# A third buffer for the modulation columns, and the gate weights of the linear attention in their stage's pool

## The chip, the core and the metric

The kernel runs on one core of a Trainium2 chip. The metric is device time in microseconds; of the kernel before there are three runs: 2583.49, 2584.60 and 2589.62, median 2584.60. One further execution was taken by the hardware profiler: 2585.34 us, of which 2583.5 us lie between its first and its last instruction (the span).

## The reference

A decoder trunk of two layers, float32, 256 tokens of width 2048. Cut to what matters here:

```python
c_act = silu(c)
for l in range(2):
    mod = c_act @ w_mod[l] + b_mod[l]                    # 2048 x 12288, one row
    shift1, scale1, gate1, shift2, scale2, gate2 = split(mod, 6)
    h = rms_norm(x, norm1_gain[l]) * (1 + scale1) + shift1
    x = x + gate1 * token_mixer(h, w_in[l], gla_w_gk[l], ..., w_out[l])
    h = rms_norm(x, norm2_gain[l]) * (1 + scale2) + shift2
    x = x + gate2 * (silu(h @ w_gate[l]) * (h @ w_up[l])) @ w_down[l]
return rms_norm(x, final_norm_gain)
```

The token mixer projects h with w_in and runs three mixers on the columns: a gated linear attention (whose gates are `lr @ gla_w_gk + gla_b_gk`, with lr of 16 columns), a sliding-window attention and a gated delta rule. Their outputs together go through w_out.

## The kernel before

Tokens stand in two blocks of 128 partitions (`blk`). Every large product is a `stream` (L293) of jobs. A job is one block of 128 rows of a weight matrix with up to 1024 of its columns (512 KB): `load` (L313) brings it into a `raw` tile (three buffers, L109), ACT rounds it to `wh` (L330), DVE forms the remainder `wl` (L331), and `products` (L342) multiplies it with both blocks of tokens, three matmuls of 512 columns for each block and half: twelve, all at L358. In some stages the weights are used whole, without rounding, and then land in the tiles raw, wh and wl in turn.

Beside this runs the modulation, which is a single row and so no matrix product: `mod_segment` (L201) cuts each of the six parts into segments of 1024 columns. A step (L208) loads 128 rows of such a segment, 512 KB, into an `mraw` tile of the pool `modp` (two buffers, L110; the load is L220), and one DVE instruction (L223) adds it, times c_act, into an accumulator `acc` (two buffers). A segment has 16 steps, which add one after another; 320 steps use mraw. The first two parts of layer 0 go through smaller tiles of other pools instead (`early`). `finish` (L228) sums each segment over the partitions with TensorE: for shift and scale by transposes (L248) and a DVE reduction (L250); for the gates it first takes two more `mraw` tiles, one for each half of 512 columns:

```python
t = tl(modp, [P, 2, 512], "mraw", F32R)
A.activation(t[:, 0], src, AF.Copy)
V.tensor_tensor(t[:, 1], src, t[:, 0].bitcast(F32), ALU.subtract)
ps = tl(psf, [P, 512], "fin")
for i in range(2):
    TE.matmul(ps, ones_r, t[:, i], start=i == 0, stop=i == 1)
```

These tiles come free when their products (L238) are through.

The text of the kernel says when a step is due: after each job, `tick` (L273) takes steps from a queue at a rate of the stage (L50 to L57: 2.0 a job beside w_out in layer 0, 0.4 and 0.25 beside the feed-forward products). The order in which each engine runs its instructions is set at build time by a scheduler: it walks the program with its own estimates of durations, lets an instruction go ahead of the text when its data and its buffer are there, and writes one fixed order for each engine. Every load is issued by SP, in one such order; a load that waits for its buffer holds back those behind it. DVE, ACT and TensorE too run in order.

The layer's shape: projection with w_in, with the delta rule and the window attention woven in; then the linear attention `gla` (L739), w_out (with `add_gated`, L928), the second norm (`norm`, L427, transposes at L444, scale and shift at L447), and the feed-forward part: products for chunks 0 to 5 in pairs of gate and up (32 jobs a pair), two halves of 24 jobs with w_down, chunks 6 to 10, and two halves of 20 jobs. A gate product's eviction is L1134, that of an up product L1138, that of w_down L929.

Before, the gate weights (`wgk`, 16 x 256) are loaded by `load_small` (L464) at a layer's start into the pool `kp`, which lives through the whole kernel. A tile `ones` of float32 ones (L163) serves a sum in the delta rule (L594) and is rounded by ACT into `ones_r` (L166) for the products L238.

Of the kernel before, what the change touches and what calls it, by code (L numbers as in the profile page):

```python
# [10 lines left out]
F32 = mybir.dt.float32  # L11
# [4 lines left out]
AF = mybir.ActivationFunctionType  # L16
# [3 lines left out]
P = 128  # L20
D = 2048
T = 256
# [81 lines left out]
def trunk(ctx: ExitStack, tc, x, cT, pos, small, consts, b_mod, w_mod, w_in, w_gk, w_out,  # L104
# [2 lines left out]

    kp = ctx.enter_context(tc.tile_pool(name="kp", bufs=1))
    rawp = ctx.enter_context(tc.tile_pool(name="rawp", bufs=3))  # L109
    modp = ctx.enter_context(tc.tile_pool(name="modp", bufs=2))  # L110
    wsp = ctx.enter_context(tc.tile_pool(name="wsp", bufs=3))
    accp = ctx.enter_context(tc.tile_pool(name="accp", bufs=2))
    gatep = ctx.enter_context(tc.tile_pool(name="gatep", bufs=2))
# [9 lines left out]
    def nm(s):  # L123
        uid[0] += 1
        return f"{s}_{uid[0]}"

    def tl(pool, shape, tag, dt=F32, bufs=None):
        return pool.tile(shape, dt, tag=tag, name=nm(tag), bufs=bufs)
# [5 lines left out]
    def bank(tag="mm"):  # L134
        if tag == "any":
            which[0] += 1
            tag = "ga" if which[0] % 3 == 0 else "mm"
        return tl(psm, [P, 512], tag, bufs=1 if tag == "ga" else 2)

    V, A, G, TE, SY = nc.vector, nc.scalar, nc.gpsimd, nc.tensor, nc.sync  # L140
# [17 lines left out]
    def cst(name):  # L158
        o, w = CONST_AT[name]
        return ct[:, o:o + w] if o < N_FULL else masks[:, o - N_FULL:o - N_FULL + w]  # L160

    ident = cst("ident")
    ones = tl(kp, [P, P], "ones")  # L163
    G.memset(ones, 1.0)
    ones_r = tl(kp, [P, P], "ones_r", F32R)
    A.activation(ones_r, ones, AF.Copy)  # L166
    eps_t = tl(kp, [P, 1], "eps")
    G.memset(eps_t, EPS)
    half = tl(kp, [P, 16], "half")
# [287 lines left out]

    scr = [None, None]

    small_t, wgk_t = {}, {}  # L460
    gains = tl(kp, [P, DEPTH, 2 * KD], "gains")
    SY.dma_start(gains, small[:, :, :2 * KD].rearrange("l p n -> p l n"))

    def load_small(l):  # L464
        small_t[l] = tl(kp, [P, SMALL_W], "small")
        SY.dma_start(small_t[l], small[l][:, 2 * KD:])
        wgk_t[l] = tl(kp, [16, 256], "wgk")
        SY.dma_start(wgk_t[l], w_gk[l])

    def sm(l, name):  # L470
        o, w = SMALL[name]
# [57 lines left out]
    def gdn(l, pool, pc, zg, cbca):  # L529
# [3 lines left out]
        for gi, name in enumerate("qkv"):  # L533
            for c2 in range(2):
                ps = bank()
# [49 lines left out]
        ps = bank()  # L585
        for ni, name in enumerate("qk"):
            for c2 in range(2):
                sq = tl(pool, [P, 2, T], "g")
                A.activation(sq, hat[name, c2], AF.Square)
                for c in range(2):  # L590
                    for blk in range(NB):
                        n = ni * 8 + blk * 4 + c2 * 2 + c
                        TE.matmul(ps[:, n:n + 1], sq[:, c, blk * P:(blk + 1) * P],
                                  ones[:, 0:1], start=True, stop=True)  # L594
        ss = tl(smp, [P, 16], "qkss")
        V.tensor_scalar(ss, ps[:, :16], EPS, None, ALU.add)
        norms = tl(smp, [P, 8], "knorm")
# [12 lines left out]
        for blk in range(NB):  # L610
            ps = bank()
# [12 lines left out]
        for blk in range(NB):  # L624
# [4 lines left out]
            ps = bank()  # L629
# [7 lines left out]
            if blk == 0:  # L637
                ps = bank()
# [6 lines left out]
            else:  # L645
                ps = bank()
# [5 lines left out]
            ps = bank()  # L652
            for h in range(4):
                TE.matmul(ps[:, h * P:(h + 1) * P], ch("k", h, blk), ch("k", h, blk),
                          start=True, stop=True)
# [3 lines left out]
            ps = bank()  # L659
            for h in range(4):  # L660
                TE.matmul(ps[:, h * P:(h + 1) * P], ch("k", h, blk), ch("q", h, blk),
                          start=True, stop=True)
# [10 lines left out]
        for m in LEVELS[1:]:  # L673
            for blk in range(NB):
                ps = bank()
# [5 lines left out]
                ps = bank()  # L681
# [13 lines left out]
        for blk in range(NB):  # L695
            rhs = v_tok[blk]
            if blk == 1:
                ps = bank()
# [7 lines left out]
            ps = bank()  # L706
# [5 lines left out]
            if blk == 0:  # L712
                ps = bank()
# [5 lines left out]
                ps = bank()  # L719
# [4 lines left out]
            else:  # L724
                ps = bank()
# [5 lines left out]
                ps = bank()  # L731
# [6 lines left out]

    def gla(l, pool, qk_tok, v_tok, zg, lr):  # L739

        chan = []
        for i in range(2):
            ps = bank("ga")
# [10 lines left out]
        ps = bank("ga")  # L754
        for blk in range(NB):
            TE.transpose(ps[:16, blk * P:(blk + 1) * P], lr[blk], ident)
        lrT = tl(pool, [16, T], "lrT", bufs=1)
        A.activation(lrT, ps[:16, :T], AF.Copy)
        ps = bank("ga")
        for blk in range(NB):  # L760
            TE.matmul(ps[:, blk * T:(blk + 1) * T], lrT[:, blk * P:(blk + 1) * P], wgk_t[l],
                      start=True, stop=True)
        z = tl(pool, [P, NB, T], "a")
        V.tensor_tensor(z, ps.rearrange("p (b c) -> p b c", b=NB), bc(sm(l, "b_gk"), NB, 1),
# [7 lines left out]
        ps = bank("ga")  # L772
# [62 lines left out]
        for blk in range(NB):  # L835
            ps = bank("ga")
            for h in range(4):
                o = ps[:, h * P:(h + 1) * P]
                if blk == 1:
                    TE.matmul(o, cross[:, h % 2, h // 2], v_tok[0][:, h * P:(h + 1) * P],  # L840
                              start=True, stop=False)
                TE.matmul(o, Am[h % 2][:, h // 2, blk], v_tok[blk][:, h * P:(h + 1) * P],
                          start=blk == 0, stop=True)
# [105 lines left out]
    def layer(l):  # L949
        wi, wo = w_in[l], w_out[l]  # L950
        load_small(l)
        blocks, at = [], 0
        for n in (K_BLOCKS if l == 0 else (KD,)):
# [90 lines left out]
        for bi, ks in enumerate(blocks):  # L1044
            first, last = bi == 0, bi == len(blocks) - 1
            rate[1] = RATE_LAST if last and l == 0 else RATE_IN[l]
            if last:
                closed.difference_update({(l, GATE1), (l, SHIFT2), (l, SCALE2)})
            for blk in range(NB):
                norm(l, 0, blk, rms[blk], h[blk], ks)  # L1050
            for name in ("qk", "z", "v"):
                project(name)
            if l == 0 and first:
                for o in range(0, n_mask, 512):
                    n = min(512, n_mask - o)
                    t = scr[1]()
                    SY.dma_start(t[:, :n], consts[:, N_FULL + o:N_FULL + o + n])
                    V.tensor_copy(masks[:, o:o + n], t[:, :n])
            if last:
                mix.clear()  # L1060
                for blk in range(NB):
                    for group in (3, 1, 2):
                        mix[blk, group] = tl(hmp, [P, 4, P], "hm")
                        G.memset(mix[blk, group][:, 0, 0:1], 0.0)
                    for name in ("gqk", "gv", "gz"):
                        G.memset(slot(hmp, "hm", (name, blk))[:, 0:1], 0.0)
                kT = swa_keys(pb, both("kv"))
                gdn(l, pg, [dict(enumerate(both(n))) for n in "qkv"], both("z"), both("cbca"))
            project("bq")
# [14 lines left out]
        for group in (3, 1, 2):  # L1084
            split_mix(l, group)
        gla(l, pw, both("gqk"), both("gv"), both("gz"), both("lr"))

        def lhs_mix(k, blk, whole):
# [129 lines left out]
```

## Time and profile before

| | before |
|---|---|
| median of three runs | 2584.60 us |
| profiled execution, whole | 2585.34 us |
| its span | 2583.5 us |
| its mean granted TensorE clock | 0.986 |
| instructions | 30803 |
| DMA, mean over the span | 233 GB/s, 600.79 MB |
| modulation steps through mraw (L223) | 320 of 512 KB, 410.3 us of DVE |

How to read it: a group's row has its line, engine, operation, the tiles written and read (out<-in), busy time, the mean of one, and the idle time before it with what ended that. SPq rows are SP issuing a load, with the time that it stood before it. The chain of waits goes back from the last instruction, at each step to what released it. PE is TensorE's matmuls, PEld its weight loads, DVE the vector engine, ACT the scalar engine, POOL GpSimd.

### The profile page before, as it was taken

The numbers are of one execution on the slowest core, as the hardware profiler recorded it, in microseconds if no ns is written. First come the engines' busy times: TensorE is split into PE (matmuls) and PEld (weight loads), VectorE is DVE, ScalarE is ACT, GpSimd is POOL, SyncE is SP. The second block draws the span as 40 slices with busy tenths as digits, with TensorE's granted clock in tenths as the row PEclk, the third lists the DMA queues.
The fourth block names the chain that finished last, engine by engine and source line by source line (L and its number), as shares of the span: only waits on it lengthen the run. The fifth ranks groups of instructions, "written<-read, shape, count | busy, mean of one in ns | idle before, by whom it ended". The sixth has DMA issues, their size and how long they took to land.

```text
span 2583.5 us, 30803 instructions
## 1 busy us (share of the span) xinstructions
PE 2432.7 (94%) x11164; PEld 1884.1 (73%) x11164; DVE 1714.4 (66%) x2171; ACT 1053.5 (41%) x1548; POOL 58.2 (2%) x117
## 2 busy tenths in 40 slices
PE   4999998889999988999999999999999999999998
PEld 2555785447878767788877878877778878888876
DVE  6767867576675777657578785888664575544555
ACT  2203443124444333344335454564644434344443
POOL 1000000000000000000000000000000000000000
PEclk9999999989999999999999999999999999999999
DMA  9996538777778888868687861675676686666654
GB/s 341 368 322 204 180 114 282 258 231 268 261 259 260 283 268 274 292 193 286 223 277 261 281 192 50 214 232 192 212 256 193 200 286 195 188 191 188 189 184 155
DMA packets 190033, 600.79 MB, mean 233 GB/s; under 512 B 21628, under 2 KB 26268, under 8 KB 189496
## 3 DMA queue, kind: packets, MB, share of 16 engines
q1 hardware_dynamic: 189880, 598.81, 70.7%
q8 instruction: 88, 1.44, 0.2%
q14 instruction: 65, 0.53, 0.1%
HBM read 596.63 MB, written 2.10 MB: 232 GB/s over the span
## 4 chain that ended last, share of the span: by engine, by line
PE 57%; DMA 20%; DVE 10%; issue 8%; ACT 4%; POOL 1%; SPq 1%; DVEq 0%; ACTq 0%; POOLq 0%
PE acc L358 48%; DMA mraw<-in_w_mod 13%; DVE wl L331 4%; DMA raw<-in_w_down 3%; DMA raw<-in_w_in 2%; DVE acc L223 2%; ACT wh L330 1%; PE mm L403 1%; PE ga L895 1%; DMA raw<-in_w_up 1%; PE mm L678 1%; PE mm L685 1%; PE ga L916 1%; DMA raw<-in_w_gate 1%; PE fin L248 1%
## 5 line engine op out<-in xcount | busy, mean ns | idle before, releaser
L358 PE MATMUL acc<-wh,hm 128*128 128x512 f32 (+3 forms) x4872 | 1339.2, 389 | 20.9 <-DVE xs L931 4.7
L330 ACT ACTIVATE wh<-raw 128x1024 fp32r<-128x1024 f32 (+3 forms) x669 | 684.7, 1025 | 985.8 <-PE acc L358 548.9
L331 DVE TENSOR_TENSOR wl<-raw,wh 128x1024 fp32r<-128x1024 f32 (+3 forms) x669 | 785.2, 1179 | 446.6 <-ACT wh L330 444.5
L358 PEld LDWEIGHTS acc<-wh,hm 128*128 128x128 f32 x4872 | 892.0, 189 | 215.8 <-issue 25.5
L358 PE MATMUL acc<-wl,hm 128*128 128x512 f32 (+3 forms) x2484 | 792.3, 394 | 12.2 <-DVE wl L331 9.7
L223 DVE SCALAR_TENSOR_TENSOR acc<-mraw,c_act,acc 128x1024 f32<-128x1024 f32 x320 | 410.3, 1282 | 225.2 <-DMA mraw<-in_w_mod 222.9
L358 PEld LDWEIGHTS acc<-wl,hm 128*128 128x128 f32 x2484 | 458.4, 190 | 124.1 <-DVE wl L331 22.3
L358 PE MATMUL acc<-wh,ahl 128*128 128x512 f32 x560 | 158.4, 397 | 0.0
L358 PEld LDWEIGHTS acc<-wh,ahl 128*128 128x128 f32 x560 | 105.8, 189 | 24.5
L358 PE MATMUL acc<-wl,ahl 128*128 128x512 f32 x280 | 90.8, 398 | 7.2 <-DVE wl L331 7.2
L223 DVE SCALAR_TENSOR_TENSOR g<-g,c_act,g 128x512 f32<-128x512 f32 x128 | 88.7, 747 | 12.6 <-DMA g<-in_w_mod 12.4
L358 PE MATMUL acc<-wh,b 128*128 128x512 f32 (+2 forms) x184 | 74.7, 545 | 2.2 <-ACT b L447 2.1
L358 PE MATMUL acc<-wl,b 128*128 128x512 f32 (+2 forms) x176 | 67.1, 518 | 2.6 <-DVE g L969 2.6
L358 PEld LDWEIGHTS acc<-wl,ahl 128*128 128x128 f32 x280 | 52.2, 189 | 23.1 <-DVE wl L331 11.3
L358 PE MATMUL acc<-raw,b 128*128 128x512 f32 (+2 forms) x176 | 67.6, 524 | 0.0
L358 PEld LDWEIGHTS acc<-wh,b 128*128 128x128 f32 x184 | 35.2, 197 | 30.8 <-issue 23.1
L358 PEld LDWEIGHTS acc<-wl,b 128*128 128x128 f32 x176 | 32.8, 192 | 29.2 <-issue 20.3
L416 ACT ACTIVATE acc<-xs 128x512 f32<-128x512 f32 x32 | 19.0, 595 | 85.7 <-DVE xs L931 85.7
L447 ACT ACTIVATE b<-mm,mod,mod 128x128 f32<-128x128 f32 x24 | 9.2, 461 | 109.7 <-DVE mod L256 92.1
L358 PEld LDWEIGHTS acc<-raw,b 128*128 128x128 f32 x176 | 33.5, 195 | 26.7 <-issue 21.7
L929 DVE TENSOR_TENSOR acc<-acc,gate 128x512 f32<-128x512 f32 x64 | 43.0, 695 | 10.3 <-PE acc L358 10.2
L358 PE MATMUL acc<-raw,hm 128*128 128x512 f32 x88 | 41.7, 598 | 1.4 <-ACT acc L416 1.4
(314 smaller groups left out, 1645.8 us busy)
## 6 DMA issues: line engine op xcount, KB each, us to landing
mraw<-in_w_mod SPq DMA_DIRECT2D x320, 512.0 KB
raw<-in_w_down SPq DMA_DIRECT2D x176, 512.0 KB
raw<-in_w_gate SPq DMA_DIRECT2D x160, 512.0 KB
raw<-in_w_up SPq DMA_DIRECT2D x160, 512.0 KB
raw<-in_w_in SPq DMA_DIRECT2D x72, 512.0 KB
g<-in_w_mod SPq DMA_DIRECT2D x128, 256.0 KB
raw<-in_w_out SPq DMA_DIRECT2D x43, 512.0 KB
raw<-in_w_in SPq DMA_DIRECT2D x32, 264.0 KB
```

Source lines behind the costliest of these rows:

```text
L223: V.scalar_tensor_tensor(acc, raw[:, a], c_act[:, i + a:i + a + 1], acc, ALU.mult, ALU.add)
L248: TE.transpose(ps[:, i * P:(i + 1) * P], acc[:, (j + i) * P:(j + i + 1) * P], ident)
L330: A.activation(wh[:, :width], raw[:, :width], AF.Copy)
L331: V.tensor_tensor(wl[:, :width], raw[:, :width], wh[:, :width].bitcast(F32), ALU.subtract)
L358: TE.matmul(ps[blk, j][:, :segs[j][2]], xa, parts[j][part], start=i == 0 and n == 0, stop=last and n == len(terms) - 1)
L403: TE.transpose(ps[:, j * P:(j + 1) * P], src[:, j * P:(j + 1) * P], ident)
L416: A.activation(scr[0]() if junk is None else junk, xs[:, blk, j * 512:(j + 1) * 512], AF.Square, accum_out=ssq[blk][:, j:j + 1])
L678: TE.matmul(ps[:, s], LT[blk][:, s], Tm[blk][:, s], start=True, stop=True)
L685: TE.matmul(ps[:, s], U[blk][:, s], m1[:, s], start=True, stop=True)
L895: TE.matmul(ps[:, j * nk:(j + 1) * nk], qT[rows, i + j], kT[rows, g, :nk], start=True, stop=True)
L916: TE.matmul(ps[:, j * 64:(j + 1) * 64], pT[:, j * nk + kb * P:j * nk + (kb + 1) * P], kv[kb][:, P + g * 64:P + (g + 1) * 64], start=kb == ...
L929: V.tensor_tensor(ps, ps, need(gate_row, (l, part, j)), ALU.mult)
```

## The change

Three edits. The pool `modp` has three buffers in place of two. The gate weights of the linear attention are no longer loaded at the layer's start into the kernel's own pool, but in `gla` into the pool of that stage. And the separate float32 ones are gone: GpSimd sets `ones_r` directly through a float32 view, and the sum in the delta rule reads the same tile.

```diff
-    modp = ctx.enter_context(tc.tile_pool(name="modp", bufs=2))
+    modp = ctx.enter_context(tc.tile_pool(name="modp", bufs=3))
...
-    ones = tl(kp, [P, P], "ones")
-    G.memset(ones, 1.0)
     ones_r = tl(kp, [P, P], "ones_r", F32R)
-    A.activation(ones_r, ones, AF.Copy)
+    G.memset(ones_r.bitcast(F32), 1.0)
...
     def load_small(l):
         small_t[l] = tl(kp, [P, SMALL_W], "small")
         SY.dma_start(small_t[l], small[l][:, 2 * KD:])
-        wgk_t[l] = tl(kp, [16, 256], "wgk")
-        SY.dma_start(wgk_t[l], w_gk[l])
...
-                                  ones[:, 0:1], start=True, stop=True)
+                                  ones_r[:, 0:1].bitcast(F32), start=True, stop=True)
...
     def gla(l, pool, qk_tok, v_tok, zg, lr):

+        wgk = tl(pool, [16, T], "wgk", bufs=1)
+        SY.dma_start(wgk, w_gk[l])
...
-            TE.matmul(ps[:, blk * T:(blk + 1) * T], lrT[:, blk * P:(blk + 1) * P], wgk_t[l],
+            TE.matmul(ps[:, blk * T:(blk + 1) * T], lrT[:, blk * P:(blk + 1) * P], wgk,
```

Lines of the changed kernel stand two lower from the ones on (L223 is L221 there, L331 is L329). Since the scheduler knows of the third buffer, it writes other orders for all engines; the number of loads is the same, and each reads the same bytes.

SP, in the feed-forward part of layer 0, where the gate product of chunks 4 and 5 follows the up product of chunks 2 and 3. In the kernel before, the mraw tiles of a finished gate segment are held there; 17 weight loads (raw) stand in a row, of which these rows show the last six, and then two columns (mraw):

```order
507 L323 DMA raw_5589<-in_w_gate 128x1024
508 L323 DMA raw_5628<-in_w_gate 128x1024
509 L323 DMA raw_5646<-in_w_gate 128x1024
510 L323 DMA raw_5667<-in_w_gate 128x1024
511 L323 DMA raw_5685<-in_w_gate 128x1024
512 L323 DMA raw_5703<-in_w_gate 128x1024
513 L220 DMA mraw_5664<-in_w_mod 128x1024
514 L220 DMA mraw_5729<-in_w_mod 128x1024
```

The changed kernel's SP in the same gate product:

```order
499 L218 DMA mraw_5827<-in_w_mod 128x1024
500 L321 DMA raw_5391<-in_w_gate 128x1024
501 L321 DMA raw_5416<-in_w_gate 128x1024
502 L218 DMA mraw_5866<-in_w_mod 128x1024
503 L321 DMA raw_5434<-in_w_gate 128x1024
504 L321 DMA raw_5455<-in_w_gate 128x1024
505 L218 DMA mraw_5923<-in_w_mod 128x1024
506 L321 DMA raw_5473<-in_w_gate 128x1024
507 L321 DMA raw_5491<-in_w_gate 128x1024
508 L218 DMA mraw_5962<-in_w_mod 128x1024
```

One column now stands ahead of every two weight loads; two of the three buffers are held there too, so each of these columns goes into the one that its predecessor has left.

TensorE, at the end of layer 0's w_out, where the second norm begins. fin is the sum of the last scale columns over the partitions, ga and mm with s as input are the norm's transposes, acc the products with w_out. Before:

```order
1065 L248 MATMUL fin_3904<-consts_88,acc_3673 128x128 x4
1066 L358 MATMUL acc_4030<-wh_4072,hm_3846 128x512
1067 L358 MATMUL acc_4029<-wl_4073,hm_3846 128x512
1068 L358 MATMUL acc_4030<-wl_4073,hm_3846 128x512
1069 L358 MATMUL acc_4029<-wh_4072,hm_3847 128x512
1070 L358 MATMUL acc_4030<-wh_4072,hm_3847 128x512
1071 L444 MATMUL ga_3922<-consts_88,s_3920 128x128 x4
```

and in the changed kernel:

```order
1040 L246 MATMUL fin_3902<-consts_88,acc_3671 128x128 x4
1041 L356 MATMUL acc_3931<-raw_3814,hm_3404 128x512
1042 L356 MATMUL acc_3932<-raw_3814,hm_3404 128x512
1043 L356 MATMUL acc_3931<-wh_3820,hm_3404 128x512
1044 L356 MATMUL acc_3932<-wh_3820,hm_3404 128x512
1045 L356 MATMUL acc_3931<-wl_3824,hm_3404 128x512
1046 L442 MATMUL ga_3848<-consts_88,s_3846 128x128 x4
```

Before, the sum stands among the first products of the feed-forward part (acc_4029), behind the norm's first transposes; now it stands among the last products with w_out (acc_3931), ahead of the norm's first transpose.

More of the change, by code (lines that the diff above doesn't have):

```diff
@@ L458, in trunk @@
     scr = [None, None]
-    small_t, wgk_t = {}, {}
+    small_t = {}
     gains = tl(kp, [P, DEPTH, 2 * KD], "gains")
```

## The prediction

> **What bounds the kernel now.** I read the page first, then the waits of the SP queue and of the engines, then windows cut by stage, and the chain of waits last.
>
> ```profile
> PE 2432.7 (94%) x11164; PEld 1884.1 (73%) x11164; DVE 1714.4 (66%) x2171; ACT 1053.5 (41%) x1548; POOL 58.2 (2%) x117
> GB/s 341 368 322 204 180 114 282 258 231 268 261 259 260 283 268 274 292 193 286 223 277 261 281 192 50 214 232 192 212 256 193 200 286 195 188 191 188 189 184 155
> PE acc L358 48%; DMA mraw<-in_w_mod 13%; DVE wl L331 4%; DMA raw<-in_w_down 3%; DMA raw<-in_w_in 2%; DVE acc L223 2%; ACT wh L330 1%; PE mm L403 1%; PE ga L895 1%; DMA raw<-in_w_up 1%; PE mm L678 1%; PE mm L685 1%; PE ga L916 1%; DMA raw<-in_w_gate 1%; PE fin L248 1%
> ```
>
> TensorE bounds most of the span, but 13% of the chain of waits is the landing of modulation columns, which feed no large product directly. The waits of the SP queue say how they get into the chain:
>
> ```profile
> SPq L220 <- DVE acc L223: 221.4, 162, 4.4
> SPq L220 <- DMA mraw<-in_w_mod: 92.2, 80, 3.6
> SPq L220 <- PE fin L238: 17.7, 10, 3.9
> ```
>
> ```profile
> DVE acc L223 <- DMA mraw<-in_w_mod: 222.9, 170, 4.0
> PE acc L358 <- DVE wl L331: 16.9, 27, 1.9
> ```
>
> SP issues every load in one order. 162 times it stood at a modulation load until DVE had used up the column two before it, 221.4 us in all, and the weight loads behind it stood too. DVE in turn stood 222.9 us for columns still in flight. One such place:
>
> ```profile
> 901.71 1.06 ACT L330 ACTIVATE wh<-raw 128x1024 fp32r<-128x1024 f32 x1 [2.84 <-DMA raw<-in_w_down]
> 902.99 1.28 DVE L223 SCALAR_TENSOR_TENSOR acc<-mraw,c_act,acc 128x1024 f32<-128x1024 f32 x1 [2.86 <-DMA mraw<-in_w_mod]
> 904.19 1.22 DVE L331 TENSOR_TENSOR wl<-raw,wh 128x1024 fp32r<-128x1024 f32 x1
> ```
>
> The rounded weights are ready at 902.77 (901.71 + 1.06), but DVE takes the remainder only at 904.19, because a column that landed late stands ahead of it in DVE's order.
>
> What this costs TensorE is read by stage. A "pair" is a gate and an up product over two chunks, 32 weight loads; a "down" is 24 loads. Windows run from one stage's first eviction (L1138 or L929) to the next's. Columns: window, length, busy time and count of PE, PEld, DVE, ACT, POOL, granted clock, DMA share, GB/s.
>
> ```profile
> 669.50:763.30 93.80, 91.58 (x405) 73.73 (x404) 63.83 (x58) 41.02 (x45) 0.96 (x1) 1.00 0.80 267
> 763.30:859.20 95.90, 92.49 (x411) 74.89 (x409) 61.57 (x56) 39.65 (x43) 0.00 (x0) 1.00 0.79 262
> 859.20:936.70 77.50, 70.35 (x306) 56.01 (x307) 54.43 (x52) 27.24 (x28) 0.95 (x1) 0.98 0.83 271
> 936.70:1013.50 76.80, 71.29 (x305) 55.72 (x304) 53.55 (x50) 25.72 (x25) 0.77 (x1) 1.00 0.85 278
> 1013.50:1107.60 94.10, 89.97 (x379) 72.91 (x379) 63.54 (x60) 35.77 (x36) 0.18 (x1) 0.96 0.81 276
> 1915.70:2004.70 89.00, 88.30 (x398) 73.24 (x399) 43.98 (x42) 37.94 (x40) 0.00 (x0) 1.00 0.65 193
> 2004.70:2097.70 93.00, 91.06 (x409) 74.83 (x407) 54.44 (x49) 39.71 (x43) 0.00 (x0) 1.00 0.74 234
> 2166.00:2233.50 67.50, 67.45 (x295) 54.89 (x294) 34.07 (x33) 26.54 (x27) 0.00 (x0) 1.00 0.60 188
> 2233.50:2321.50 88.00, 87.49 (x386) 71.91 (x385) 43.82 (x41) 35.85 (x37) 0.00 (x0) 1.00 0.63 191
> ```
>
> The same windows for line L223 alone give the modulation steps in each (DVE's count); the others of layer 1 have none:
>
> ```profile
> 669.50:763.30 93.80, 20.55 (x16) 1.00 0.80 267
> 763.30:859.20 95.90, 19.19 (x15) 1.00 0.79 262
> 859.20:936.70 77.50, 20.61 (x17) 0.98 0.83 271
> 936.70:1013.50 76.80, 20.49 (x16) 1.00 0.85 278
> 1013.50:1107.60 94.10, 20.58 (x17) 0.96 0.81 276
> 2004.70:2097.70 93.00, 11.44 (x9) 1.00 0.74 234
> ```
>
> A pair without steps takes 88.5 us (mean of 89.0 and 88.0), a down without them 67.5. The six stages with 90 steps are longer by 5.3, 7.4, 10.0, 9.3, 5.6 and 4.5 us, 42.1 together: 0.33 to 0.50 us per step in a pair, 0.59 in a down. That is the pool of the first term.
>
> **The change, part by part.** *Start.* A table load and the rounding of the ones go.
>
> ```profile
> 2.03 0.31 ACT L166 ACTIVATE ones_r<-ones 128x128 fp32r<-128x128 f32 x1
> ...
> 10.22 0.63 ACT L416 ACTIVATE b<-xs 128x512 f32<-128x512 f32 x1 [4.05 <-DMA xs<-in_x]
> ```
>
> ACT waits 4.05 us for x anyway, so this is worth 0; the gate weights' issue that leaves SP's start is shorter still. Without that cover it would be 0.31 us and the load.
>
> *Gate weights.* Their load now stands among layer 0's last in_w_in loads (SP order) and is first read here:
>
> ```profile
> 394.34 0.33 SPq L323 DMA_DIRECT2D raw<-in_w_in  x1
> ...
> 412.32 1.13 PE L761 MATMUL ga<-wgk,lrT 16*128 16x256 f32 x4
> ```
>
> The last in_w_in load is issued 18 us before (394.34), and in the new order the gate weights' load stands ahead of that one, so I take 0. What it waits for on ACT, the squares of the first gated output, is over by then. Without that cover it costs one landing, about 4 us a layer by the column landings below.
>
> *The order alone.* DVE's order of the changed kernel holds 19, 21, 8, 13 and 16 steps in the five layer-0 stages above, 15 in layer 1's first pair, which had none, and none in its second. At 0.40 a step in pairs (row mean; 5.6 kept where the count hardly moves) and 0.59 in downs: 7.6 + 8.4 + 4.7 + 7.7 + 5.6 + 6.0 = 40.0 against 42.1, so -2.
>
> *The third buffer, where all three serve the stream.* 30 of these 92 steps are the exception treated next. The other 62, at the same prices, cost some 27 us. If late columns and the blocked queue are their whole cause, 27 go; if it is traffic, none. I take 40%, -11: in the rows at 901 to 904 both show, ACT waiting 2.84 for its own weights and DVE 2.86 for a column.
>
> *One buffer left.* `finish` of a gate segment takes two mraw buffers until its products L238. With two buffers the stream then stops:
>
> ```profile
> 754.88 39.56 SPq L323 DMA_DIRECT2D raw<-in_w_gate  x15
> ```
>
> 15 weight loads, no column. With three it goes on through one buffer, one column per two weight loads (order above), 14 steps in layer 0 and 16 in layer 1. Each waits for the step just before it. The price is the buffer's turn-round, landing + DVE step + reissue, against two loads' TensorE time, 2 x 88.5/32 = 5.53 us. Rows of the chain, each the next use of a buffer (between the first two stands one more, between the last two five):
>
> ```profile
> 173.97 4.09 DMA mraw<-in_w_mod
> ...
> 184.88 3.95 DMA mraw<-in_w_mod
> ...
> 803.88 3.56 DMA mraw<-in_w_mod
> ...
> 852.18 5.72 DMA mraw<-in_w_mod
> ```
>
> That is 5.46 us a turn in the first stretch, which would cost nothing, and 8.05 in the second, which would cost 2.5 us each time. One column at a time brings less traffic than the second stretch's, so I keep the 0.40 used above (12 us), nearest the first.
>
> *End of layer 0's attention.* The last two scale sums move ahead of the second norm (PE order above). Now:
>
> ```profile
> 517.08 1.09 PE L248 MATMUL fin<-consts,acc 128*128 128x128 f32 x4 [5.88 <-DVE acc L223]
> ```
>
> ```profile
> 574.34 1.50 ACT L447 ACTIVATE s<-mm,mod,mod 128x128 f32<-128x128 f32 x4 [5.79 <-DVE mod L256]
> ```
>
> ```profile
> 516.70:581.30 64.60, 53.18 (x148) 27.68 (x149) 47.68 (x67) 19.18 (x48) 3.01 (x4) 0.87 0.70 231
> ```
>
> TensorE stands 5.88 us for the steps, and ACT 5.79 for the last scales. Bounds: +6 (the sums stand earlier, and stall once more) to -14 (both waits, and 2 of the 8.4 us that the clock of 0.87 takes from 64.6). I take -8: the first wait, and part of the second, since the norm's own chain stays. The Trainium skill, "TensorE: Matmul & The Clock Gate", section "Part 1: The HAM clock gate", says that about 3.4 us without work halve the clock for a window; by it a vanished stall is worth an estimated further 1.7 us, and the 0.87 beside stalls of this size agrees.
>
> Layer 1's attention keeps its stages and nearly its steps (61 for 58 up to its end, by DVE's order): 0, within 5 either way.
>
> **Sum.** The profiled execution took 2585.3 us (span 2583.5), 0.7 above the median. 2585.3 - 2 - 11 - 8 = 2564.3: I say 2564.
>
> **Rivals.** *One-buffer stretches block SP: slower.* SP stands at a column until its predecessor's step ends, and two weight loads stand behind it. For it: the turns of 8.05 us. Against: the 5.46. At 7.0 us a turn, 30 x (7.0 - 5.53) = 44 replace the 12 counted: 2564 + 32 = 2596. Above 6.6 us the whole gain of 21 is gone.
>
> *Traffic is the limit: no change.* A third column in flight only lengthens the queue: -2 from the order, nothing else, 2583. For it: DMA shares of 0.83 and 0.85 in the downs. Against: such a down moves 24 + 16 loads of 512 KB, 21.0 MB, which at the 368 GB/s of the second slice takes 57 us, not the 76.8 seen. The Trainium skill, "DMA: Bandwidth & Descriptors", section "Where 436 GB/s comes from", puts the memory's limit per core at about 358 GB/s; that would be 59 us, an estimate, below TensorE's 67.5 too, and the 368 lies above it.
>
> *All of it goes: faster still.* -2 - 27 - 14: 2542. For it: the bytes of a dense down leave the DMA idle a quarter of its time (57 of 76.8 us), so its 9 us can be waiting alone. Against: raw itself has three buffers, and still ACT waits 2.84 us for it above.
>
> That the buffers change nothing is excluded by the order.
>
> **Numbers.** Forecast (2552 to 2576) 0.50; all goes 0.13; traffic 0.17; blocked queue 0.20, of which 0.03 end within 8 us of no change. A measurement of this kernel tells about 0.3% (8 us) from no change. Faster (below 2577) 0.63, same 0.20, slower 0.17. The range takes in 2542 and 2596: 2540 to 2597, with about 0.1 left out at each end.
>
> **What would show it.** Right: the SP waits of the column loads on DVE fall from 221 us to under 120, DVE's for columns to under 150, the downs of layer 0 below 74 us, and the stall at the sums before 520 is gone. Wrong: the pairs with one-buffer stretches (layer 0's second, layer 1's first) take over 97 us (blocked queue), or the downs keep their 0.59 us a step (traffic). What I can't read from an order is when a sum that stands earlier is ready; a new stall of PE at L248's place would spoil the third term.

## The result, and the profile after

| | before | after |
|---|---|---|
| median | 2584.05 us (4 runs, 2578.14 to 2589.62) | 2552.72 us (4 runs, 2545.96 to 2560.67) |
| ratio | | 0.9874, 95% interval 0.9848 to 0.9901 |
| profiled execution | 2585.34 us, span 2583.5 | 2549.07 us, span 2547.1 |
| mean granted clock | 0.986 | 0.990 |

The change is faster by 31 us by the medians, by 36 between the two profiled executions. The forecast was 21.

First the page of the changed kernel, the line of busy times:

```profile
PE 2422.7 (95%) x11164; PEld 1881.8 (74%) x11164; DVE 1715.0 (67%) x2171; ACT 1052.3 (41%) x1546; POOL 57.3 (2%) x117
```

TensorE runs as many matmuls as before, 11164, and is busy 10.0 us less (2432.7 before). The work is the same, so this is the clock, and the granted clock fits it: 0.986 of 2583.5 leaves out 36 us, 0.990 of 2547.1 leaves out 25. What is left of the span, TensorE's idle time, falls from 2583.5 - 2432.7 = 150.8 to 2547.1 - 2422.7 = 124.4 us, by 26.4. Together 36.4, the whole difference of the spans.

The waits of the changed kernel: of SP's queue, of DVE and of TensorE (us in total, times, the longest). L218 is the column load, L221 the step, L329 the remainder, L356 the product.

```profile
SPq L218 <- DVE acc L221: 189.5, 140, 5.1
SPq L218 <- DMA mraw<-in_w_mod: 59.3, 47, 7.2
...
DVE acc L221 <- DMA mraw<-in_w_mod: 154.1, 130, 4.2
...
PE acc L356 <- DVE wl L329: 7.8, 17, 1.2
```

DVE's waits for columns fell by 69 us (from 222.9), SP's at the columns only by 32 (from 221.4). TensorE's waits for a remainder are less than half of the 16.9 they were.

The stages of the feed-forward part, after, with line L221 alone (DVE's time and number of steps, granted clock, DMA share, GB/s); the five of layer 0 that the prediction showed, then the first two pairs of layer 1:

```profile
644.30:738.30 94.00, 24.45 (x20) 1.00 0.84 286
738.30:834.70 96.40, 26.93 (x22) 0.98 0.84 288
834.70:904.50 69.80, 10.26 (x9) 0.98 0.73 246
904.50:975.20 70.70, 16.75 (x14) 1.00 0.85 288
975.20:1065.00 89.80, 20.53 (x16) 1.00 0.83 284
1877.10:1970.90 93.80, 19.36 (x16) 0.96 0.78 256
1970.90:2060.90 90.00, 0.00 (x0) 1.00 0.65 192
```

These seven take 604.5 us; before they took 93.8 + 95.9 + 77.5 + 76.8 + 94.1 + 89.0 + 93.0 = 620.1. The two downs give 13.8 of the 15.6, and they are the stages that lost steps: 17 and 16 have become 9 and 14. The pairs ahead of them have four and seven more, and take no more time worth the name.

The larger piece lies ahead of the first gate product's eviction. The same view for all engines (busy time and count of PE, PEld, DVE, ACT, POOL, clock, DMA share, GB/s), from the first eviction of layer 0's w_out to that eviction, before:

```profile
475.20:624.20 149.00, 129.17 (x402) 75.06 (x403) 99.56 (x116) 39.33 (x76) 4.68 (x6) 0.92 0.72 238
```

and after:

```profile
465.60:596.00 130.40, 121.25 (x395) 69.08 (x394) 88.61 (x107) 39.07 (x74) 4.70 (x6) 0.99 0.69 244
```

This stage is 18.6 us shorter. TensorE's idle time in it fell from 149.00 - 129.17 = 19.8 to 9.2 us, by 10.7, and its busy time by 7.9. Seven of the 402 matmuls lie outside the window now; most of the 7.9 is the clock, which rose from 0.92 to 0.99. The view of TensorE by time shows the stalls that went. Before, at the second norm (behind the 5.88 us at 517 that the prediction shows):

```profile
562.25 1.11 PE L444 MATMUL ga<-consts,s 128*128 128x128 f32 x4 [4.34 <-DVE s L441]
...
574.70 0.66 PE L444 MATMUL ga<-consts,s 128*128 128x128 f32 x4 [0.23 <-DVE s L441]
...
577.98 0.67 PE L444 MATMUL mm<-consts,s 128*128 128x128 f32 x4 [2.17 <-DVE s L441]
579.89 1.08 PE L444 MATMUL ga<-consts,s 128*128 128x128 f32 x4 [1.24 <-DVE s L441]
```

and after, the whole list of waits over 1.1 us from 466 to 596:

```profile
504.43 0.75 PE L246 MATMUL fin<-consts,acc 128*128 128x128 f32 x4 [3.52 <-DVE sums L248]
...
553.77 0.63 PE L442 MATMUL mm<-consts,s 128*128 128x128 f32 x4 [2.33 <-DVE s L439]
```

The rows of before also show how the clock is read from durations: the same four transposes take 1.11 us right behind the stall of 4.34, and 0.66 at 574.70.

The rest of the 36.4: 9.6 us up to the first eviction of w_out (475.2 to 465.6), and the other way 3.0 us in layer 0's first up product (45.3 to 48.3), 2.9 in layer 1's attention (511.2 to 514.1) and 1.5 in the up product behind it (46.6 to 48.1).

### The profile page after: what moved, and what is told of

The parts are those of the page before. It is cut to its first block, busy times and chain, and to the rows that moved or that the text cites. A ratio compares the mean times of both kernels' runs of the same rounds, so it can differ in the third digit from the quotient of the medians.

```text
span 2547.1 us, 30770 instructions
## 1 busy us (share of the span) xinstructions
PE 2422.7 (95%) x11164; PEld 1881.8 (74%) x11164; DVE 1715.0 (67%) x2171; ACT 1052.3 (41%) x1546; POOL 57.3 (2%) x117
## 5 line engine op out<-in xcount | busy, mean ns | idle before, releaser
L356 PE MATMUL acc<-wh,hm 128*128 128x512 f32 (+3 forms) x4872 | 1333.4, 388 | 17.3 <-ACT acc L414 5.1
L329 DVE TENSOR_TENSOR wl<-raw,wh 128x1024 fp32r<-128x1024 f32 (+3 forms) x669 | 785.7, 1179 | 464.2 <-ACT wh L328 461.0
L356 PEld LDWEIGHTS acc<-wh,hm 128*128 128x128 f32 x4872 | 890.7, 189 | 212.4 <-issue 20.3
L356 PE MATMUL acc<-wl,hm 128*128 128x512 f32 (+3 forms) x2484 | 793.3, 394 | 6.2 <-DVE wl L329 4.8
L356 PEld LDWEIGHTS acc<-wl,hm 128*128 128x128 f32 x2484 | 458.3, 189 | 116.2 <-issue 18.7
L221 DVE SCALAR_TENSOR_TENSOR acc<-mraw,c_act,acc 128x1024 f32<-128x1024 f32 x320 | 410.1, 1282 | 156.8 <-DMA mraw<-in_w_mod 154.1
L356 PE MATMUL acc<-wh,ahl 128*128 128x512 f32 x560 | 157.8, 396 | 0.0
L356 PEld LDWEIGHTS acc<-wh,ahl 128*128 128x128 f32 x560 | 105.6, 189 | 24.5
L221 DVE SCALAR_TENSOR_TENSOR g<-g,c_act,g 128x512 f32<-128x512 f32 x128 | 88.7, 746 | 11.5 <-DMA g<-in_w_mod 11.5
L356 PE MATMUL acc<-wl,ahl 128*128 128x512 f32 x280 | 90.7, 397 | 3.0 <-DVE wl L329 3.0
L356 PE MATMUL acc<-wh,b 128*128 128x512 f32 (+2 forms) x184 | 72.8, 535 | 2.2 <-ACT b L445 2.1
L356 PE MATMUL acc<-raw,b 128*128 128x512 f32 (+2 forms) x176 | 66.6, 517 | 0.0
L356 PE MATMUL acc<-wl,b 128*128 128x512 f32 (+2 forms) x176 | 66.1, 512 | 0.2 <-DVE g L967 0.2
L356 PEld LDWEIGHTS acc<-wl,ahl 128*128 128x128 f32 x280 | 52.6, 189 | 17.2 <-DVE wl L329 5.2
L356 PEld LDWEIGHTS acc<-wh,b 128*128 128x128 f32 x184 | 34.8, 194 | 31.7 <-issue 23.6
L356 PEld LDWEIGHTS acc<-wl,b 128*128 128x128 f32 x176 | 32.6, 190 | 26.7 <-issue 21.5
L356 PEld LDWEIGHTS acc<-raw,b 128*128 128x128 f32 x176 | 32.7, 190 | 26.1 <-issue 21.8
L210 POOL MEMSET acc<- 128x1024 f32 x20 | 19.0, 954 | 1019.4 <-PE fin L246 709.7
L929 DVE TENSOR_TENSOR xs<-xs,acc 128x512 f32<-128x512 f32 x64 | 41.6, 678 | 0.1
```

Source lines behind the costliest of these rows:

```text
L210: G.memset(st["acc"][:, :width], 0.0)
L221: V.scalar_tensor_tensor(acc, raw[:, a], c_act[:, i + a:i + a + 1], acc, ALU.mult, ALU.add)
L329: V.tensor_tensor(wl[:, :width], raw[:, :width], wh[:, :width].bitcast(F32), ALU.subtract)
L356: TE.matmul(ps[blk, j][:, :segs[j][2]], xa, parts[j][part], start=i == 0 and n == 0, stop=last and n == len(terms) - 1)
L929: V.tensor_tensor(x_j, x_j, ps, ALU.add)
```

## The experiments

All are made from the changed kernel. Ratios are to the kernel before, run beside them.

**The small edits alone.**

```diff
-    modp = ctx.enter_context(tc.tile_pool(name="modp", bufs=3))
+    modp = ctx.enter_context(tc.tile_pool(name="modp", bufs=2))
```

> The changed kernel with two buffers for the modulation columns again: only the gate weights' place and the single set of ones are left of the change. If the third buffer makes the gain (theory), this takes the time of the kernel before, 2584 us within 6, the SP waits of the column loads on DVE are back near 221 us, and the first gate eviction of layer 0 is back near 624 us. If the gate weights' place, or the order that the scheduler writes when it is there, makes a part of it (rival), it is at 2570 or below, and the first gate eviction of layer 0 comes before 615.

Measured: 2585.41 us, ratio 1.0015 [0.9995, 1.0035]; SP's waits 223.6 us, first gate eviction at 616.1. The gate weights' place and the single set of ones are worth nothing that shows, with two buffers; the third buffer makes the gain. The eviction came 8 us sooner than in the profile of before, all but 1.6 of it ahead of w_out's first eviction (468.7 against 475.2): small changes of the order, and chance, move this point by that much between single executions.

**Three buffers in one half of layer 0 only.** A spare `mraw` tile is taken at the second norm and kept to the end:

```diff
+    spare = []
...
+                if l == 0:
+                    spare.append(tl(modp, [P, 1024], "mraw"))
+                    G.tensor_copy(spare[0][:, 0:1], hold[0])
...
+    G.tensor_copy(spare[0][:, 0:1], xs[:, NB - 1, D - 1:D])
```

or it is taken at the start and given free at the second norm:

```diff
+    spare = [tl(modp, [P, 1024], "mraw")]
+    G.memset(spare[0][:, 0:1], 0.0)
...
+                if l == 0:
+                    G.tensor_copy(spare[0][:, 0:1], hold[0])
```

> The changed kernel, but one of the three buffers of the columns is taken out for good at layer 0's second norm: three buffers up to the end of layer 0's attention, two from there on. Theory of two separate parts: the gain up to layer 0's first gate eviction (28 us in the profiled runs) stays, the rest of the kernel goes as before, with downs of 76 to 78 us: 2552 to 2560. Rival, that layer 0's attention only moves work into the feed-forward part and this part would give it back: 2570 to 2584. Rival, that the feed-forward part makes nearly all: 2575 to 2584.

> The mirror of it: one of the three buffers of the columns is held from the start and given free at layer 0's second norm; two buffers in layer 0's attention, three from there on. Theory of two separate parts: the first gate eviction of layer 0 stays near 624 us as before, the downs of layer 0 take 70 to 71 us each, and the whole is 2566 to 2576. Rival, that the feed-forward part makes nearly all of the gain: 2552 to 2560. Rival, that it makes nothing by itself: 2580 to 2588.

Measured: three early 2559.46 us, 0.9904 [0.9879, 0.9929]; three late 2575.53 us, 0.9967 [0.9951, 0.9983]. Both as the theory of two separate parts has it: 0.96 and 0.33% make 1.29, and the whole change gave 1.26, each to within 0.2 or 0.3. The stage from w_out's first eviction to the first gate eviction, line L221 alone, with three early:

```profile
468.00:600.60 132.60, 37.29 (x30) 0.96 0.69 239
```

and with three late:

```profile
472.10:620.30 148.20, 48.74 (x38) 0.92 0.71 241
```

The same view of the two kernels compared gives, for before,

```profile
475.20:624.20 149.00, 48.74 (x38) 0.92 0.72 238
```

and, for after,

```profile
465.60:596.00 130.40, 37.29 (x30) 0.99 0.69 244
```

So much is shown: with a third buffer eight steps of the 38 are through before the stage begins, DVE has 11.5 us less to do in it, and it is 16 to 19 us shorter. That the eight steps are the cause was argued from this, and a kernel further down, with two buffers, shows that they are not all of it. The downs of layer 0 go with their steps too. Three early, then two:

```profile
833.40:909.80 76.40, 20.59 (x17) 0.94 0.81 275
909.80:985.30 75.50, 20.43 (x16) 1.00 0.84 281
```

**The gate sums without the columns' buffers.** `finish` of a gate segment holds two `mraw` tiles. With two buffers for the columns, those tiles get a pool of their own (the memory is that of the changed kernel):

```diff
-    modp = ctx.enter_context(tc.tile_pool(name="modp", bufs=3))
+    modp = ctx.enter_context(tc.tile_pool(name="modp", bufs=2))
+    finp = ctx.enter_context(tc.tile_pool(name="finp", bufs=1))
...
-                    t = tl(modp, [P, 2, 512], "mraw", F32R)
+                    t = tl(finp, [P, 2, 512], "ft", F32R)
```

or no tile at all, one float32 product from the accumulator, with two buffers and with three:

```diff
-                    t = tl(modp, [P, 2, 512], "mraw", F32R)
-                    A.activation(t[:, 0], src, AF.Copy)
-                    V.tensor_tensor(t[:, 1], src, t[:, 0].bitcast(F32), ALU.subtract)
                     ps = tl(psf, [P, 512], "fin")
-                    for i in range(2):
-                        TE.matmul(ps, ones_r, t[:, i], start=i == 0, stop=i == 1)
+                    TE.matmul(ps, ones_r.bitcast(F32), src, start=True, stop=True)
```

> Two buffers for the columns, and the rounded halves of a gate segment's sum in a buffer of their own, so that the stream of columns never stops at such a sum; the memory taken is that of the changed kernel. If the depth of the stream makes the gain (theory), little of it is here: 2575 to 2590, with the first gate eviction of layer 0 near 624, since the waits up to there have no gate sum beside them in the new order that frees a column. If what counts is that the stream is not stopped by the gate sums (rival), it is within 6 us of the changed kernel, 2547 to 2559, and the downs of layer 0 take 70 to 71 us each.

> Two buffers for the columns, and a gate segment is summed over the partitions by one float32 product straight from its accumulator, so that no sum takes a column buffer and no buffer of its own either. With the run before that kept the stream going through the gate sums (2559 us with two buffers) this separates what the sums take from what the depth gives. Theory that the stops at the gate sums are the larger part of the gain: 2552 to 2562, with downs of 70 to 71 us in layer 0. Rival, that the place in memory or the order by chance made that run: 2570 or more.

> The same with three buffers, so that the stream always has all three. If depth and the sums' hold on the buffers are two separate costs, this is below both kernels: 2535 to 2548, the one-buffer stretches are gone and the pairs of layer 0 take 90 to 94 us. If one buffer more is enough for either (the third buffer and the freed sums do the same thing), it is the changed kernel's time, 2548 to 2558.

Measured, as a table of two by two:

| | two buffers | three buffers |
|---|---|---|
| gate sums take column buffers | 2585.41 us, 1.0015 [0.9995, 1.0035] | 2552.72 us, 0.9874 [0.9848, 0.9901] |
| own pool | 2559.06 us, 0.9905 [0.9881, 0.9929] | not built: takes 4 KB a partition more than the changed kernel |
| from the accumulator | 2566.27 us, 0.9935 [0.9907, 0.9962] | 2541.06 us, 0.9833 [0.9805, 0.9862] |

The theory that depth makes nearly all of the gain fell with the first of these: with two buffers, and the stream only kept from stopping at the gate sums, 0.95 of the 1.26% are there. The second lies between its two expectations, with 0.65%. Depth and freed sums each give a good part alone. Together they give 1.67% here and 1.44 when measured again below, where the two alone make 1.26 + 0.65 = 1.91; with intervals of 0.3 each, that they add up to less is likely, not shown.

The last kernel of the left column also tests the eight steps. With two buffers, and nothing held, 31 steps are left in the stage from w_out's first eviction to the first gate eviction, nearly the 30 of three buffers:

```profile
470.80:611.60 140.80, 126.35 (x399) 72.41 (x398) 89.86 (x109) 39.79 (x76) 4.68 (x6) 0.94 0.67 226
```

The stage takes 140.8 us, 8.2 less than before, where the changed kernel has 130.4. Seven steps out of the stage so go with less than half of the gain; the rest came only with three buffers (127.6 to 132.6 us in the five profiles that have them there, with 28 to 30 steps), and what it is made of stays open. The sums' own pool leaves 31 steps too, and takes 144.8 us, with thirty more matmuls in the window. Behind that stage, two buffers with freed sums lose nothing: from the first gate eviction to the end the kernel with the sums' own pool takes 2558.3 - 610.1 = 1948.2 us, the changed kernel 2547.1 - 596.0 = 1951.1, and the kernel before 2583.5 - 624.2 = 1959.3.

The steps in the downs of layer 0, gate sums in their own pool and two buffers:

```profile
850.60:921.50 70.90, 6.32 (x6) 0.98 0.64 214
921.50:992.40 70.90, 16.81 (x14) 1.00 0.84 285
```

So a down takes 70.9 us with two buffers too, if the pairs before it have taken the steps; and the pairs can, once the stream isn't stopped. The waits of this kernel, where L222 is the step and L219 the column load:

```profile
DVE acc L222 <- DMA mraw<-in_w_mod: 188.1, 157, 3.6
...
SPq L219 <- DVE acc L222: 242.2, 170, 5.2
```

SP stands longer at the columns than before the change (242.2 against 221.4), and the profiled execution is 25 us shorter all the same (2560.31): what SP's row adds up is not what the stream costs. With three buffers and nothing held, the pairs and downs of layer 0:

```profile
638.20:734.40 96.20, 29.59 (x24) 1.00 0.86 298
734.40:830.60 96.20, 25.66 (x20) 1.00 0.83 290
830.60:901.10 70.50, 5.05 (x4) 0.98 0.64 210
901.10:970.70 69.60, 16.74 (x14) 1.00 0.84 290
```

The time was as expected, the pairs were not: 90 to 94 us were expected, 96.2 came. Its gain over the changed kernel is earlier: the first gate eviction stands at 590.3, where the changed kernel has 596.0.

**Side by side.** The changed kernel and this last one once more, on one chip.

> The changed kernel once more, side by side with the next one, and a second profile of the same order of instructions. Two readings are open. If the 93.8 us of layer 1's first pair are the price of its one-buffer stretch, they come again, 92.5 to 95. If they were a half-clock stretch that a stall of 3.7 us happened to bring, the pair takes 89 to 91 here. The time: 2549 to 2557.

> Three buffers and gate sums straight from the accumulator, beside the changed kernel on one chip. If the gate sums' hold on two of three buffers still costs something, this is 8 to 16 us below the changed kernel and its interval lies apart from it. If the 12 us seen between separate calls were chance, the two are within 5 us.

Measured: 2550.34 us, 0.9868 [0.9842, 0.9893], and 2545.03 us, 0.9856 [0.9831, 0.9881]. Run beside each other, the two can't be told apart. All runs of both, measured on more than one chip, ten of the one (mean 2550.7) and nine of the other (2544.1), are 6.7 us apart, with a 95% interval of 2.3 to 11.0 by their spread: the best version here is probably the one with three buffers and the sums from the accumulator, by a quarter of a per cent. The second profile of the changed kernel settles layer 1's first pair:

```profile
1885.40:1974.40 89.00, 88.25 (x397) 73.22 (x398) 62.31 (x57) 38.46 (x41) 0.00 (x0) 1.00 0.82 276
```

89.0 us, as without any step, at the same order and the same one-buffer stretch that took 93.8 in the first profile. There TensorE had stood once, longer than in the second profile (1.44 us at the same line), and the clock fell with it (0.96 in that stage):

```profile
1877.86 1.11 PE L401 MATMUL mm<-consts,s 128*128 128x128 f32 x4 [3.68 <-DVE s L1136]
```

**Steps due earlier, two buffers.**

```diff
-    modp = ctx.enter_context(tc.tile_pool(name="modp", bufs=3))
+    modp = ctx.enter_context(tc.tile_pool(name="modp", bufs=2))
...
-RATE_OUT = (2.0, 0.4)
+RATE_OUT = (2.6, 0.4)
```

> Two buffers and the gate sums as before (the small edits alone, which by themselves gave no difference), but the steps beside layer 0's product with w_out are due at 2.6 a job in place of 2.0, so that the last scale sums stand ahead of the second norm on TensorE, as in the changed kernel. If the place of the sums is what the third buffer changed at the end of layer 0's attention (theory), the first gate eviction of layer 0 comes at 596 to 606 in the profile and the time is 2555 to 2568, with the feed-forward part as before. If the depth itself serves it (rival), the steps only crowd the loads of w_out: first gate eviction 614 or later, 2575 to 2590.

Measured: 2580.23 us, 0.9985 [0.9967, 1.0004], first gate eviction at 624.1. The theory fell. The sums do stand ahead of the second norm, but 36 steps are still in the stage:

```profile
479.50:624.10 144.60, 46.19 (x36) 0.96 0.71 239
```

and TensorE still waits, only at other places:

```profile
560.67 0.63 PE L246 MATMUL fin<-consts,acc 128*128 128x128 f32 x4 [2.48 <-DVE acc L221]
...
567.33 0.66 PE L442 MATMUL ga<-consts,s 128*128 128x128 f32 x4 [1.30 <-DVE s L439]
```

A sum's place in the order is no gain while its columns come no sooner.

**The columns issued by GpSimd**, with two buffers, with three, and with three and the sums from the accumulator:

```diff
-            SY.dma_start(raw, w_mod[l, i * P:(i + n) * P, c0:c0 + width]
+            (SY if early else G).dma_start(raw, w_mod[l, i * P:(i + n) * P, c0:c0 + width]
```

> Two buffers and the gate sums as before, but the columns' loads through mraw are issued by GpSimd in its own queue, so that a column that waits for its buffer no longer holds the weight loads behind it on SP. It separates the two ways in which the shallow stream can cost: the blocked queue and the late column on DVE. If the blocked queue is the larger part (theory), 2552 to 2568, with the downs of layer 0 at 74 us or less. If the late columns are (rival), DVE still waits some 215 us for columns, and the time is 2574 to 2590.

> The changed kernel with the columns' loads issued by GpSimd. If three buffers still leave a cost of the blocked queue (SP stood 189 us at columns), 2535 to 2548. If the third buffer has taken the queue's part already and what is left is the late columns, 2548 to 2560. Should GpSimd's own work behind the columns (the weights of the linear attention, L889 there) come late, layer 0's attention gets longer and the time is above 2560.

> Three buffers, gate sums straight from the accumulator, and the columns issued by GpSimd: all three causes taken away together. If they add up, 2522 to 2537, the lowest time here. If the stream is served by three free buffers, the queue adds nothing: 2536 to 2548, as with three free buffers on SP.

Measured: 2670.50 us, 1.0329 [1.0284, 1.0374]; 2655.70 us, 1.0283 [1.0254, 1.0312]; 2671.45 us, 1.0329 [1.0295, 1.0364]. They lie 85, 103 and 130 us above the same kernels with SP issuing (2585.41, 2552.72 and 2541.06). The first and the third were expected nowhere near. For the second, a time above 2560 was named, with a longer attention in layer 0; that came (first gate eviction at 630.3 against 596.0), but it is a third of the loss. SP's queue was free of the columns in all three, so a queue blocked on SP can't be what made them slow. DVE's and TensorE's waits with two buffers:

```profile
DVE acc L221 <- DMA mraw<-in_w_mod: 232.6, 183, 7.3
...
PE acc L356 <- DVE wl L329: 45.7, 41, 5.3
```

TensorE waits for remainders 45.7 us where it waited 16.9, and 59.3 in the kernel with nothing held. One place, from the kernel with nothing held (L325 is the remainder there, L352 the product):

```profile
652.99 1.28 DVE L221 SCALAR_TENSOR_TENSOR acc<-mraw,c_act,acc 128x1024 f32<-128x1024 f32 x1 [3.63 <-DMA mraw<-in_w_mod]
654.19 1.22 DVE L325 TENSOR_TENSOR wl<-raw,wh 128x1024 fp32r<-128x1024 f32 x1
...
655.47 0.99 PE L352 MATMUL acc<-wl,hm 128*128 128x512 f32 x2 [2.64 <-DVE wl L325]
```

It is the pattern that the prediction showed at 901 us, only worse: the remainder stands behind a column that hasn't landed. The runs don't separate a blocked queue from late columns. The other queue changed every engine's order; the issue itself takes 0.53 us there (median of 320) against 0.33 on SP; GpSimd stood 879.6 us with two buffers at columns whose buffer DVE still held, and its own work behind them; and the columns' transfers went through a queue of another kind, as the page for two buffers says (packets, MB, share of 16 engines):

```profile
q1 hardware_dynamic: 143800, 431.02, 48.3%
q0 software_dynamic: 46080, 167.79, 19.6%
```

They do show, at single places, that a late column on DVE holds TensorE with SP free. They don't show that this is the loss: with three buffers and nothing held, DVE waited 146.8 us for columns in all, where the same kernel with SP issuing waited 140.8 and is 130 us faster. Most of the loss stays open.

## Why the prediction came out as it did

*The direction, and the small edits at nothing: right.* The small edits alone measure 1.0015 with 1 inside the interval. The size was too small by a third: 21 us forecast, 31 measured, and 2552.72 is just inside the lower end of the range with the even chance (2552 to 2576).

*Feed-forward part, -2 for the order and -11 for the third buffer: the sum was right (-13; the seven stages gave -15.6, and -20.9 in the second profile), its split was not.* That the sum fits is partly luck: the 40% of the third buffer's term was a choice with no row behind it. (62 steps at the prices given come to 40.0 - 12 = 28 us, not 27; 40% of either is 11.) I gave each step a fixed price, 0.59 us in a down. The runs show no fixed price. Downs with 16 or 17 steps take 75.5 to 77.5 us (before, small edits, three buffers early; 74.0 once, with the steps due earlier). Those with 14 or fewer take 69.4 to 71.4 in every kernel whose columns SP issues, with two buffers as with three, and no less with 4 or 5 steps than with 14; with GpSimd issuing they take 69.0 to 74.3. No kernel had 16 steps there with three buffers, so that the number alone decides is likely, not shown. Against a down without steps, 67.5, a step costs 0.59 us in the one and (69.8 + 70.7 - 2 x 67.5)/23 = 0.24 in the other. The order, which I put at -2, is the gain there, and the third buffer is what let the scheduler write it; with two buffers, freed sums did so too. Why 16 steps cost so much more than 14 is not settled.

*The one-buffer stretches, kept at 0.40 a step: they cost less.* Layer 1's 16 steps, 6.4 us in my sum, cost 0.5 (89.0 against 88.5) where no stall fell in. Layer 0's second pair takes 96.4 with two buffers held and 96.2 with none. That they would not cost more than the 0.40 was right, and the rival that had them block SP gave 2596.

*End of layer 0's attention, -8: the term that was mis-sized, by more than half.* The stage gave -18.6 us in the first profile and 149.0 - 131.5 = -17.5 in the second, beyond my bound of -14. I took the stall at the sums and some of the wait behind it, and of the 8.4 us that the clock took there I counted 2, in the bound alone. The idle time fell by 10.7 us, and the busy time by another 7.9, most of it the clock. The failed step was to count the waits by name at two rows, and so to leave out the clock and what DVE would no longer have to do in that stage: eight steps, 11.5 us. The two-buffer kernel with 31 steps in the stage says that these steps are less than half of it; the rest of the 18 us is measured, and its cause open.

*Ahead of it there was no term.* 9.6 us came there in the profiles. Single executions put w_out's first eviction at 475.2, 468.7 and 472.1 us with two buffers (before, small edits, three late) and at 465.6, 469.0 and 468.0 with three (after, again, three early): 4.5 us on the mean. The changed kernel alone, in one and the same order, gave 465.6 and 469.0. So a part of the 36 us of the profiled pair is probably chance, which the 31 of the medians agrees with, and whether the third buffer is worth something there is not settled.

*Layer 1's attention, 0 within 5.* +2.9 in the first profile, +8.0 in the second (from 1316.2 to 1835.4, 519.2 us against 511.2). What it is made of stays open.

*The signs.* The downs below 74 us came (69.8, 70.7). The stall before 520, 5.88 us for the steps, is gone, but one of 3.52 stands in its place: there a sum waits for DVE's reduction of the one before it, which frees the one buffer of the sums' pool (L119). DVE's waits for columns, to be under 150, reached 154.1. SP's, to be under 120, stayed at 189.5, a sign that I should not have chosen: the sums' own pool shows 242.2 beside a faster kernel. No pair with a one-buffer stretch passed 97 us in the changed kernel (96.4 and 96.0, 93.8 and 89.0 in its two profiles; one took 97.7 with three buffers late), and the downs did not keep their 0.59.

*The rivals.* "All of it goes" (2542) was nearer the result than "traffic is the limit" (2583), and no further from it than the forecast: 10.7 us to 11.3. The second down moves 288 GB/s with 14 steps where it moved 278 with 16, at the same DMA share of 0.85 and in 6.1 us less: the 278 were no limit.

## What to carry to other kernels

Where a background stream shares an engine with the main work, count its steps in each stage before and after: a deeper buffer moved steps out of the stages where that engine is waited for, and a fixed price per wait misses this. Then look for a run that moves the steps without the depth; here it gave less than half of what the stage gained. Look for who else takes tiles from the stream's pool: keeping two short-lived tiles out of it was worth 0.65 or 0.95%, where the third buffer was worth 1.26. And when a stall of TensorE goes, read its busy time too: the same matmuls in fewer microseconds are the clock, here 10.0 of 36.4 us, and 7.0 of 32.9 in the second profile (busy 2425.7, span 2550.6).

## What the runs showed of the hardware

The clock's answer to a stall is not the same each time. In three executions with the same order of TensorE up to there, TensorE stood 2.33, 2.31 and 2.33 us at the same transposes of the second norm. The 10 us around it (window, length, busy time and count of PE, PEld, DVE, ACT, POOL, granted clock, DMA share, GB/s), in the changed kernel:

```profile
552.00:562.00 10.00, 6.53 (x34) 4.97 (x34) 4.67 (x10) 8.16 (x22) 0.56 (x1) 1.00 0.01 2
```

in its second profile:

```profile
555.20:565.20 10.00, 7.62 (x34) 5.98 (x34) 4.66 (x10) 7.71 (x22) 0.56 (x1) 0.83 0.00 2
```

and with three buffers early:

```profile
550.80:560.80 10.00, 7.68 (x28) 6.14 (x29) 3.97 (x9) 6.83 (x18) 0.56 (x1) 0.66 0.00 1
```

The clock in these 10 us is 1.00, 0.83 and 0.66. If it is either full or half, as the four transposes at 1.11 and 0.66 us above suggest, that is half speed for none, 3.4 or 6.8 of the 10 us. The Trainium skill, "TensorE: Matmul & The Clock Gate", section "Part 1: The HAM clock gate (the "warmup" mystery)", has a free-running window of 3413 ns, so that the answer depends on where in it the stall lies; the three agree with that. It also puts the throttled state behind at least one idle window, and here a stall of 2.3 us was enough. A stall's price is then a chance, and this is likely a part of why single runs of one kernel lie 15 to 25 us apart: of the ten runs of the small edits alone, the fastest (2572.16 us) has a mean clock of 0.987 and the slowest (2596.98) one of 0.981.
